# Spreading the running sums of a Mamba-2 head group over the partitions: matmuls into PSUM, or DMAs from a scratch in HBM

## The chip, the cores and the metric

The kernel runs on one core of a Trainium2 chip. The metric is the device time of one execution in microseconds (us), the median of several runs. The engines are TensorE (PE; its weight loads are listed apart as PEld), VectorE (DVE), ScalarE (ACT), GpSimd (POOL) and SyncE (SP), which here issues nearly all DMAs.

## The reference, cut to what matters

The model is a decoder trunk of two layers, 256 tokens, width 2048, in float32. Each layer normalises its input and projects it to the columns of an attention group and of a state-space (SSM) group; both outputs are normalised and mapped by one output projection.

```python
for l in range(DEPTH):                       # DEPTH = 2
    h = rmsnorm(x, norm_w)
    proj = h @ w_in                          # 2048 x 11856
    ... attention part (NSA), output y_attn ...
    xbc = silu(causal_depthwise_conv(xbc, conv_w, conv_b))
    xs, bm, cm = split(xbc)
    dt = softplus(dt + dt_bias); a = -exp(a_log)          # 32 heads
    # SSD, one chunk of 256 tokens, 8 groups of 4 heads
    cum   = cumsum(dt * a, axis=tokens)                   # (256, 32)
    decay = exp(where(causal, cum[l] - cum[s], -inf))     # (l, s, head)
    y = ((c @ b.T)[..., None] * decay) @ (xs * dt)
    y_ssm = grouped_rmsnorm((y + d_skip * xs) * silu(z), norm_ssm_w)
    x = x + concat(y_attn, y_ssm) @ w_out
return rmsnorm(x, final_norm_w)
```

The change is about `decay`: for each of 32 heads the kernel needs, on partition s and for all l, the difference of two running sums.

## The kernel before, in words

**Weight stream.** The weights of both projections are cut into tiles of 128 x 1024 (512 KB), 252 a layer. One tile is one *slot*. SyncE loads it into a ring of five buffers `wr` (line 147, issued in program order when VectorE has freed the oldest). ScalarE rounds it to `wh` (float32r, line 118), VectorE subtracts to get the rest `wl` (line 121); both run two slots ahead of TensorE (LH = LL = 2), each in a ring of four. In a slot TensorE (line 133) does eight pairs of matmuls: `wh` with 512 columns, then `wl` with 256. Two slots with 16 x 128 rows of input make one column tile in PSUM (`ppj`); it is evacuated in the next slot (`evac`, line 312).

**Side work.** All other work stands in generators that are resumed once per slot by `tick` (line 297); `yield from W(k)` lets WAITS[k] slots pass. So the order of the instructions on each engine is written out by hand, and a side instruction of TensorE stands between two slots of the stream.

**The SSM stage.** The column tiles come in the order `gd` (gates and dt), then for each of eight groups g: C, B, x, x, z, z, twelve slots a group. `gd_side` (line 369) makes dt, multiplies it by -exp(a_log) and takes the running sums by a matmul with a triangle (lines 409, 410): 32 heads on partitions, 256 tokens along them. It copies them to `cT` (tile `rt`) and, split into a rounded part and a rest, to the 64 rows of `cum2` (tile `PC`, lines 413 to 417); transposed they go to `cs`, 128 tokens on partitions. When the second z tile of group g is there, `ssm_side(g)` starts (line 816). It makes the products c b (`cb`, PSUM `b1`), transposes x (line 465), and then for each of its four heads spreads the running sums over all 128 partitions with a matmul: the stationary operand is a column of `eR`, a 64 x 32 pattern of ones, broadcast to 128 columns; the moving one is `cum2`; the result is `pc`, 4 x 256 columns in PSUM `b2` (line 471). ScalarE takes Relu(cs - pc) into `E` (tile `B`, a ring of two; lines 481, 482), then Exp of it; VectorE and GpSimd multiply by the masked `cb`; TensorE makes `py`, the last reader of `E` (line 495).

The lines that the change touches:

```python
cum2 = C["cum2"] = sb([96, 256], "PC", F32R)[0:64]
act(cum2[0:32], ps[0:32, :256])
lo(cum2[32:64], cT, cum2[0:32])
mm(pc[:, hh], eR[:, 4 * g + hh:4 * g + hh + 1].to_broadcast([64, 128]), C["cum2"], True, True)
act(E[:, hh, 0:256], pc[:, hh], AF.Relu, scale=-1.0, bias=cs[:, 0, c:c + 1])
```

The tag `B` also holds attention tiles later in the layer, and `PC` also an attention tile; `b2` also takes the sums of the compression and attention scores.

The other entries of the wait table that matter: from the start of `ssm_side` to its transposes 5 slots (W0 to W3), to the Relus 2 more (W5), to the Exp 2 (W9), to `py` 2 (W11); in `gd_side` the sums are copied in layer 0 at slot 18, in layer 1 earlier.

Of the kernel before, what the change touches and what calls it, by code (L numbers as in the profile page):

```python
# [11 lines left out]
F32 = mybir.dt.float32  # L12
F32R = mybir.dt.float32r
I32 = mybir.dt.int32
AF = mybir.ActivationFunctionType
# [70 lines left out]
def body(ctx: ExitStack, tc: tile.TileContext, wst, w1, xin, pos, w2, par, con, y):  # L86
    nc = tc.nc
# [3 lines left out]

    pp = ctx.enter_context(tc.tile_pool(name="pp", bufs=1))
    qq = ctx.enter_context(tc.tile_pool(name="qq", bufs=1, space=bass.MemoryType.PSUM))
    ctx.enter_context(tc.manual_schedule())

    cnt = [0]

    def sb(shape, tag, dt=F32, bufs=1):
        cnt[0] += 1
        return pp.tile(shape, dt, tag=tag, name=f"{tag}_{cnt[0]}", bufs=bufs)  # L100

    def pst(tag, shape=(128, 512), bufs=1):
        cnt[0] += 1
        return qq.tile(list(shape), F32, tag=tag, name=f"p{tag}_{cnt[0]}", bufs=bufs)

    def W(k):
        for _ in range(WAITS[k]):
            yield
# [3 lines left out]
    def act(out, in_, f=AF.Copy, **kw):  # L112
        if f in (AF.Ln, AF.Exp) and table[0] != AF.Exp:
            ACT.preload_act_table_set("natural_log_exp_and_others")  # L114
            table[0] = AF.Exp
        elif f in (AF.Silu, AF.Sin):
            table[0] = f
        ACT.activation(out, in_, f, **kw)  # L118
# [10 lines left out]
    def lo(out, full, hi):  # L129
        tt(out, full, f(hi), OP.subtract)  # L130

    def mm(out, lhsT, rhs, start, stop):
        PE.matmul(out, lhsT, rhs, start=start, stop=stop, skip_group_check=True)  # L133
# [67 lines left out]
    i4 = cst[:, C_I4:C_I4 + 32]  # L201
# [50 lines left out]

    one = sb([128, 1], "one", F32R)
    onr = one.to_broadcast([128, 128])
    eR = sb([64, 32], "eR", F32R)

    KT = [sb([128, 2, 2, 272], f"KT{g}", F32R) for g in range(2)]
    VC = [sb([96, 2, 128], f"VC{g}", F32R) for g in range(2)]
    PC = [None]
# [5 lines left out]
    cs = sb([128, 2, 32], "cs")  # L265
# [28 lines left out]
    sides = []  # L294
# [43 lines left out]
    h = [None] * NK  # L338
# [16 lines left out]
    for L in range(DEPTH):  # L355
# [4 lines left out]
        C = {}  # L360
# [8 lines left out]
        def gd_side(G):  # L369
# [2 lines left out]
            rmul(G)  # L372
            if L == 0:
                act(one, ones[:, 0:1])
                act(eR, i4[0:64])
            yield from W(27)
            if L == 0:
                sides.append(rope_tables())
# [29 lines left out]
            ps = pst("t", bufs=2)  # L408
# [1 line left out]
            mm(ps[0:32, 128:256], z[:, 1, :], tri, False, True)  # L410
            yield from W(36)
            cT = sb([128, 256], "rt")[0:32]
            cum2 = C["cum2"] = sb([96, 256], "PC", F32R)[0:64]
            act(cum2[0:32], ps[0:32, :256])
            act(cT, ps[0:32, :256])
            yield from W(37)
            lo(cum2[32:64], cT, cum2[0:32])
            ps = pst("t", bufs=2)
            for b in range(2):
                PE.transpose(ps[:, b * 32:b * 32 + 32], cT[:, b * 128:b * 128 + 128], ident[0:32, 0:32])  # L420
# [10 lines left out]
        def conv_side(U, dst, ct):  # L431
# [10 lines left out]
            for tap in (2, 1, 0):  # L442
                s = 3 - tap
                stt(dst[:, s:], U[:, :256 - s], w[:, tap:tap + 1], dst[:, s:], OP.mult, OP.add)

        def ssm_side(g, CV):
            yield from W(0)
            act(CV, CV, AF.Silu)
# [17 lines left out]
            yield from W(4)  # L466
            while "gd" not in C:
                yield
            pc = pst("b2", (128, 1024)).rearrange("p (h l) -> p h l", h=4)
            for hh in range(4):  # L470
                mm(pc[:, hh], eR[:, 4 * g + hh:4 * g + hh + 1].to_broadcast([64, 128]), C["cum2"], True, True)
            E = sb([128, 1536], "B", bufs=2).rearrange("p (h l) -> p h l", h=4)
            cbm = reg[:, 1536:1920]
            tt(cbm, cb[:, :384], mk3, OP.mult)
            xdt = reg[:, 2048:2560].rearrange("p (b h c) -> p b h c", b=2, h=4)
# [2 lines left out]
            yield from W(5)  # L478
            for hh in range(4):
                c = 4 * g + hh  # L480
                act(E[:, hh, 0:256], pc[:, hh], AF.Relu, scale=-1.0, bias=cs[:, 0, c:c + 1])
                act(E[:, hh, 256:384], pc[:, hh, 128:256], AF.Relu, scale=-1.0, bias=cs[:, 1, c:c + 1])
                if hh < 3:
                    yield from W(6 + hh)
            yield from W(9)
# [305 lines left out]
        def on_coltile(kind, i, ps):  # L791
# [21 lines left out]
            elif kind == "z":  # L813
                evac(ps, C["CV"][:, 4 + i % 2])
                if i % 2:
                    sides.append(ssm_side(i // 2, C["CV"]))
            elif kind in ("kc", "vc"):
                if i == 0 and kind == "kc":
                    C["w2"] = sb([128, 4, 128], "za")
# [241 lines left out]
```

## Time and profile before

| | |
|---|---|
| time, median of 3 runs | 1636.64 us (1636.07 to 1638.41) |
| profiled execution, first to last instruction (span) | 1634.5 us |
| TensorE busy | 1605.6 us, 98% |
| VectorE, ScalarE, GpSimd busy | 77%, 65%, 20% |
| DMA moved | 286.28 MB, mean 175 GB/s |
| DMA queue 1 (SyncE), share of 16 engines | 51.5% |

The profiled execution's own time is its span, 1634.5 us, and what lies before the first and after the last instruction, which the page does not list; the runs' median is 2.1 us above the span. Matmul durations are latencies and overlap, so how fast TensorE goes is read from start to start. A tile's name is followed by what it was made from: `pb<-PC,eR` is a matmul into PSUM `b2` that reads `PC` and `eR`. Names starting with p are PSUM.

### The profile page before, as it was taken

How to read it: one execution, taken by the hardware profiler on the slowest of the kernel's cores; microseconds unless marked ns; L12 is line 12 of the kernel's file. 1: busy time of each engine (PE TensorE's matmuls, PEld its weight loads, DVE VectorE, ACT ScalarE, POOL GpSimd, SP SyncE). 2: the span in 40 equal slices, each digit the busy share in tenths (PEclk: the TensorE clock that was granted, in tenths of full speed). 3: DMA queues.
4: the chain of work that ended last, by engine and by line, in shares of the span. 5: the costliest groups of instructions: out<-in, count | busy, mean ns of one | idle time of the engine just before them, and what ended most of it. 6: DMA issues, size and time to landing. Idle time of an engine off the chain costs nothing.

```text
span 1634.5 us, 26127 instructions
## 1 busy us (share of the span) xinstructions
PE 1605.6 (98%) x9590; PEld 1380.9 (84%) x9590; DVE 1263.6 (77%) x2224; ACT 1058.7 (65%) x1911; POOL 323.5 (20%) x342
## 2 busy tenths in 40 slices
PE   8999999999999999999999999999999999999996
PEld 6888888888888888888888888888788888888885
DVE  7878888877778788776677778788858878878654
ACT  5577767755677777545457777777557777765452
POOL 2222222221112222001112222222201212220011
PEclk8999999999999999999999999999999999999998
DMA  7545445477443444555555554545854443445552
GB/s 258 174 156 177 168 168 175 167 252 269 150 142 131 161 138 153 187 195 187 182 179 180 169 168 159 175 156 200 288 202 146 145 149 130 155 168 183 186 193 83
DMA packets 83777, 286.28 MB, mean 175 GB/s; under 512 B 9329, under 2 KB 9713, under 8 KB 83649
## 3 DMA queue, kind: packets, MB, share of 16 engines
q1 hardware_dynamic: 83376, 283.77, 51.5%
q8 instruction: 75, 1.23, 0.3%
q0 software_dynamic: 272, 0.84, 0.2%
q14 instruction: 54, 0.43, 0.1%
HBM read 282.48 MB, written 2.10 MB: 174 GB/s over the span
## 4 chain that ended last, share of the span: by engine, by line
PE 84%; ACT 8%; DVE 6%; issue 1%; DMA 1%; SPq 0%; DVEq 0%; ACTq 0%
PE ppj L133 75%; PE po L133 3%; PE pb L133 3%; ACT A L118 3%; ACT wh L118 2%; DVE wl L121 1%; DVE A L121 1%; ACT L114 1%; ACT L118 1%; PE pt L133 1%; DVE sm L121 1%; ACT PC L118 1%; DVE rt L121 1%; PE pt L465 0%; PE pt L726 0%
## 5 line engine op out<-in xcount | busy, mean ns | idle before, releaser
L121 DVE TENSOR_TENSOR wl<-wr,wh 128x1024 fp32r<-128x1024 f32 x503 | 624.6, 1251 | 206.3 <-ACT wh L118 205.6
L133 PE MATMUL ppj<-h,wh 128*128 128x512 f32 x1984 | 707.2, 400 | 7.7 <-DVE h L124 6.0
L133 PE MATMUL ppj<-s,wh 128*128 128x512 f32 x1984 | 703.1, 399 | 1.7 <-DVE za L121 1.7
L118 ACT ACTIVATE wh<-wr 128x1024 fp32r<-128x1024 f32 x503 | 522.4, 1047 | 112.0 <-PE ppj L133 89.2
L133 PE MATMUL ppj<-h,wl 128*128 128x256 f32 x1984 | 555.1, 280 | 0.0
L133 PE MATMUL ppj<-s,wl 128*128 128x256 f32 x1984 | 552.8, 279 | 0.0
L133 PEld LDWEIGHTS ppj<-h,wh 128*128 128x128 f32 x1984 | 373.4, 188 | 103.2 <-DVE h L124 7.9
L133 PEld LDWEIGHTS ppj<-s,wh 128*128 128x128 f32 x1984 | 372.4, 188 | 95.1 <-DVE za L121 3.3
L133 PEld LDWEIGHTS ppj<-h,wl 128*128 128x128 f32 x1984 | 375.1, 189 | 0.1
L133 PEld LDWEIGHTS ppj<-s,wl 128*128 128x128 f32 x1984 | 373.5, 188 | 0.1
L310 POOL TENSOR_TENSOR uu<-uu,rr 128x256 f32<-128x256 f32 x120 | 103.6, 864 | 576.3 <-DVE uu L121 555.3
L118 ACT ACTIVATE ev<-ppj 128x256 f32<-128x256 f32 x184 | 70.3, 382 | 189.1 <-PE ppj L133 184.9
L121 DVE TENSOR_TENSOR xT<-xT,ppj 128x256 f32<-128x256 f32 x128 | 53.8, 421 | 31.7 <-PE ppj L133 29.2
L118 ACT ACTIVATE A<-A,nm 128x128 f32<-128x128 f32 (+2 forms) x192 | 75.4, 394 | 0.9 <-DVE nm L661 0.4
L310 POOL TENSOR_TENSOR za<-za,rr 128x256 f32<-128x256 f32 x34 | 43.3, 1274 | 138.9 <-DVE za L121 115.4
L118 ACT ACTIVATE ev<-xT 128x256 f32<-128x256 f32 x30 | 12.6, 418 | 86.0 <-DVE xT L121 86.0
L121 DVE TENSOR_TENSOR uu<-ppj,ev 128x256 f32<-128x256 f32 x118 | 49.6, 420 | 23.6 <-ACT ev L118 22.9
L661 DVE CUSTOM_DVE_ANT_0 A<-pb,con 128x128 f32<-128x128 f32 (+2 forms) x192 | 44.1, 293 | 26.1 <-PE pt L729 25.6
L292 POOL TENSOR_TENSOR SQ<-SQ,ev 128x256 f32<-128x256 f32 x28 | 20.7, 741 | 218.8 <-ACT ev L118 218.8
L118 ACT ACTIVATE A<-A,sm 128x256 f32<-128x256 f32 x64 | 27.3, 498 | 46.9 <-DVE sm L121 46.9
L124 DVE SCALAR_TENSOR_TENSOR att<-uu,par,att 128x255 f32<-128x255 f32 (+2 forms) x96 | 55.6, 580 | 2.3
L124 DVE SCALAR_TENSOR_TENSOR A<-uu,par,A 128x255 f32<-128x255 f32 (+2 forms) x96 | 55.3, 576 | 2.3
(199 smaller groups left out, 1512.7 us busy)
## 6 DMA issues: line engine op xcount, KB each, us to landing
wr<-wst SPq DMA_DIRECT2D x500, 512.0 KB, 3.6
V<-w SPq DMA_DIRECT2D x64, 256.0 KB, 4.1
xT<-xin SPq DMA_DIRECT2D x4, 512.0 KB, 7.6
y<-xT SPq DMA_DIRECT2D x7, 256.0 KB, 2.9
za<-w POOLq DMA_DIRECT2D x2, 256.0 KB, 3.6
con<-con SPq DMA_DIRECT2D x1, 417.5 KB, 10.3
y<-xT SPq DMA_DIRECT2D x2, 128.0 KB, 1.7
par<-par SPq DMA_DIRECT2D x1, 184.0 KB, 3.6
```

Of the source, the lines that this page charges most:

```text
L114: ACT.preload_act_table_set("natural_log_exp_and_others")
L118: ACT.activation(out, in_, f, **kw)
L121: DVE.tensor_tensor(out, a, b, op=op)
L124: DVE.scalar_tensor_tensor(out, a, s, b, op0=op0, op1=op1)
L133: PE.matmul(out, lhsT, rhs, start=start, stop=stop, skip_group_check=True)
L292: POOL.tensor_tensor(sq[0], sq[0], t, op=OP.add)
L310: POOL.tensor_tensor(dst, dst, rr[0], op=OP.mult)
L661: DVE.tensor_tensor_reduce(out=o, in0=i, in1=m, op0=OP.add, op1=OP.min, scale=SC, scalar=3e38, accum_out=acc)
```

## The change

The running sums are written once per layer, as 32 rows of 256 floats, to a scratch in HBM (`cum`, 32 KB, a ring of two over the layers). For each group a new side `spread_side(g)`, started when the first x tile of the group is evacuated (slot 12g + 8 of the layer), waits until the scratch exists in the program and issues two DMAs on SyncE's queue straight into the group's `E`: the four rows of the group, read with a step of zero over the 128 partitions, 256 columns of each head, and then the last 128 columns again for the second block. `ssm_side` takes this `E`, and the Relus work in place. The four spreading matmuls, `eR`, `cum2` and `pc` go; `cT` and `cs` stay.

```diff
--- before.py
+++ after.py
@@ -91,6 +91,7 @@
 
     pp = ctx.enter_context(tc.tile_pool(name="pp", bufs=1))
     qq = ctx.enter_context(tc.tile_pool(name="qq", bufs=1, space=bass.MemoryType.PSUM))
+    dd = ctx.enter_context(tc.tile_pool(name="dd", bufs=1, space=bass.MemoryType.DRAM))
     ctx.enter_context(tc.manual_schedule())
 
     cnt = [0]
@@ -252,7 +253,6 @@
 
     one = sb([128, 1], "one", F32R)
     onr = one.to_broadcast([128, 128])
-    eR = sb([64, 32], "eR", F32R)
 
     KT = [sb([128, 2, 2, 272], f"KT{g}", F32R) for g in range(2)]
     VC = [sb([96, 2, 128], f"VC{g}", F32R) for g in range(2)]
@@ -372,7 +372,6 @@
             rmul(G)
             if L == 0:
                 act(one, ones[:, 0:1])
-                act(eR, i4[0:64])
             yield from W(27)
             if L == 0:
                 sides.append(rope_tables())
@@ -410,11 +409,10 @@
             mm(ps[0:32, 128:256], z[:, 1, :], tri, False, True)
             yield from W(36)
             cT = sb([128, 256], "rt")[0:32]
-            cum2 = C["cum2"] = sb([96, 256], "PC", F32R)[0:64]
-            act(cum2[0:32], ps[0:32, :256])
             act(cT, ps[0:32, :256])
+            cum = C["cum"] = dd.tile([32, 256], F32, tag="cum", name=f"cum_{L}", bufs=2)
+            nc.sync.dma_start(cum, cT)
             yield from W(37)
-            lo(cum2[32:64], cT, cum2[0:32])
             ps = pst("t", bufs=2)
             for b in range(2):
                 PE.transpose(ps[:, b * 32:b * 32 + 32], cT[:, b * 128:b * 128 + 128], ident[0:32, 0:32])
@@ -442,6 +440,19 @@
             for tap in (2, 1, 0):
                 s = 3 - tap
                 stt(dst[:, s:], U[:, :256 - s], w[:, tap:tap + 1], dst[:, s:], OP.mult, OP.add)
+
+        def spread(g):
+            E = C["E", g] = sb([128, 1536], "B", bufs=2).rearrange("p (h l) -> p h l", h=4)
+            cum = C["cum"]
+            for to, a, b in ((0, 0, 256), (256, 128, 256)):
+                src = bass.AP(tensor=cum.tensor, offset=cum.offset + 1024 * g + a,
+                              ap=[[0, 128], [256, 4], [1, b - a]])
+                nc.sync.dma_start(E[:, :, to:to + b - a], src)
+
+        def spread_side(g):
+            while "cum" not in C:
+                yield
+            spread(g)
 
         def ssm_side(g, CV):
             yield from W(0)
@@ -466,10 +477,7 @@
             yield from W(4)
             while "gd" not in C:
                 yield
-            pc = pst("b2", (128, 1024)).rearrange("p (h l) -> p h l", h=4)
-            for hh in range(4):
-                mm(pc[:, hh], eR[:, 4 * g + hh:4 * g + hh + 1].to_broadcast([64, 128]), C["cum2"], True, True)
-            E = sb([128, 1536], "B", bufs=2).rearrange("p (h l) -> p h l", h=4)
+            E = C["E", g]
             cbm = reg[:, 1536:1920]
             tt(cbm, cb[:, :384], mk3, OP.mult)
             xdt = reg[:, 2048:2560].rearrange("p (b h c) -> p b h c", b=2, h=4)
@@ -478,8 +486,8 @@
             yield from W(5)
             for hh in range(4):
                 c = 4 * g + hh
-                act(E[:, hh, 0:256], pc[:, hh], AF.Relu, scale=-1.0, bias=cs[:, 0, c:c + 1])
-                act(E[:, hh, 256:384], pc[:, hh, 128:256], AF.Relu, scale=-1.0, bias=cs[:, 1, c:c + 1])
+                act(E[:, hh, 0:256], E[:, hh, 0:256], AF.Relu, scale=-1.0, bias=cs[:, 0, c:c + 1])
+                act(E[:, hh, 256:384], E[:, hh, 256:384], AF.Relu, scale=-1.0, bias=cs[:, 1, c:c + 1])
                 if hh < 3:
                     yield from W(6 + hh)
             yield from W(9)
@@ -814,6 +822,8 @@
                 evac(ps, C["CV"][:, 4 + i % 2])
                 if i % 2:
                     sides.append(ssm_side(i // 2, C["CV"]))
+                else:
+                    sides.append(spread_side(i // 2))
             elif kind in ("kc", "vc"):
                 if i == 0 and kind == "kc":
                     C["w2"] = sb([128, 4, 128], "za")
```

## Rows read from the trace of the kernel before

**Rows 1.** The page's first part: busy us, share of the span, instructions.

```profile
PE 1605.6 (98%) x9590; PEld 1380.9 (84%) x9590; DVE 1263.6 (77%) x2224; ACT 1058.7 (65%) x1911; POOL 323.5 (20%) x342
```

**Rows 2.** Six groups as stretches, busiest and sum: busy us (x), PEclk, DMA share, GB/s.

```profile
151.87:189.50 37.63, 37.63 (x227) 32.23 (x225) 32.81 (x52) 27.49 (x43) 9.53 (x10) 1.00 0.52 168
...
sum 225.43, PE 225.43 PEld 193.21 DVE 188.64 ACT 168.13 POOL 55.24; mean PE 37.57 PEld 32.20 DVE 31.44 ACT 28.02 POOL 9.21
```

**Rows 3.** Chain of waits from 80 to 340 us, shares by line.

```profile
by line: PE ppj L133 90.8%; PE po L133 3.9%; PE pb L133 3.5%; PE pt L465 1.2%; PE pt L133 0.6%
```

**Rows 4.** All that reads eR: ns min/median/max, first and last start, form.

```profile
L133 PE MATMUL pb<-PC,eR x64: 271/276/383, 79.6 to 1140.4; 64*128 64x256 f32 x64
```

**Rows 5.** Timeline of TensorE, layer 0, group 0: start us, us, what.

```profile
79.02 0.27 PE L133 MATMUL ppj<-h,wl 128*128 128x256 f32 x1
...
79.36 0.28 PE L133 MATMUL ppj<-h,wl 128*128 128x256 f32 x1
79.58 0.72 PE L133 MATMUL pb<-PC,eR 64*128 64x256 f32 x4
...
80.57 0.28 PE L133 MATMUL ppj<-h,wl 128*128 128x256 f32 x1
```

**Rows 6.** Timeline of TensorE, the transposes of group 0.

```profile
76.24 0.62 PE L465 MATMUL pt<-con,A 128*128 128x128 f32 x4
...
76.94 0.28 PE L133 MATMUL ppj<-h,wl 128*128 128x256 f32 x1
```

**Rows 7.** Timeline of TensorE, the transposes of group 4.

```profile
226.79 0.62 PE L465 MATMUL pt<-con,A 128*128 128x128 f32 x4
227.35 0.73 PE L133 MATMUL pb<-PC,eR 64*128 64x256 f32 x4
...
228.34 0.28 PE L133 MATMUL ppj<-h,wl 128*128 128x256 f32 x1
```

**Rows 8.** Groups of ScalarE by shape: busy us, mean ns, idle before.

```profile
L118 ACT ACTIVATE ev<-ppj 128x256 f32<-128x256 f32 x184 | 70.3, 382 | 189.1 <-PE ppj L133 184.9 <-DVE att L393 1.9 <-DVE wl L121 1.9
...
L118 ACT ACTIVATE A<-A,nm 128x256 f32<-128x256 f32 x64 | 31.6, 495 | 0.0
L118 ACT ACTIVATE B<-pb,cs 128x256 f32<-128x256 f32 x64 | 31.3, 489 | 5.6 <-PE pb L133 5.6
...
L118 ACT ACTIVATE ev<-xT 128x256 f32<-128x256 f32 x30 | 12.6, 418 | 86.0 <-DVE xT L121 86.0
```

**Rows 9.** Who waited for whom, 114 to 340 us: total us, times, longest.

```profile
DVE wl L121 <- ACT wh L118: 21.1, 17, 3.0
```

**Rows 10.** DMA queues: 1624.4:1626.4 (q1), 17.5:18.1 and 17.5:19.3 us (q0): packets, MB, share.

```profile
q1 hardware_dynamic: 288, 0.26, 39.0%
...
q0 software_dynamic: 14, 0.06, 57.5%
...
q0 software_dynamic: 48, 0.13, 31.4%
```

**Rows 11.** Costliest conversions (mean ns of one), and SyncE's own waits.

```profile
L121 DVE TENSOR_TENSOR wl<-wr,wh 128x1024 fp32r<-128x1024 f32 x503 | 624.6, 1251 | 206.3 <-ACT wh L118 205.6
...
L118 ACT ACTIVATE wh<-wr 128x1024 fp32r<-128x1024 f32 x497 | 519.0, 1052 | 112.0 <-PE ppj L133 89.2 <-issue 20.0 <-DMA wr<-wst 2.3
...
SPq L147 <- DVE wl L121: 819.6, 307, 8.7
```

**Rows 12.** DMA queue 1 of the whole run, and issues: KB each, us to landing.

```profile
q1 hardware_dynamic: 83376, 283.77, 51.5%
...
wr<-wst SPq DMA_DIRECT2D x500, 512.0 KB, 3.6
...
y<-xT SPq DMA_DIRECT2D x2, 128.0 KB, 1.7
```

**Rows 13.** Timeline of ScalarE, layer 0: the running sums and the first Relus.

```profile
69.84 0.36 ACT L118 ACTIVATE rt<-pt 32x256 f32<-32x256 f32 x1
...
83.65 2.60 ACT L118 ACTIVATE B<-pb,cs 128x256 f32<-128x256 f32 x8
```

## The prediction

> **What bounds the kernel now.** The first part of the page says how much each engine works: TensorE is busy for 1605.6 of 1634.5 us, VectorE 77%, ScalarE 65% [rows 1]. Averages can hide stages, so the next view is the table of stretches over six SSM head groups, the stage that the change touches: TensorE is busy in every microsecond of 225.43, at the full granted clock (1.00, the 2.4 GHz level), while VectorE has 31.4 and ScalarE 28.0 us of work in a group's 37.6 [rows 2]. The chain of waits over the same stage has nothing but TensorE in it [rows 3]. So in this stage each microsecond taken out of TensorE's stream is a microsecond off the end, as long as nothing else becomes late, and work added elsewhere costs nothing as long as it stays inside its slack. That leaves two questions: what the removed matmuls cost as TensorE issues them, and whether the weights still come in time.
>
> **What goes from TensorE.** Per group and layer four matmuls `pb<-PC,eR` with 64 rows and 256 columns, 64 in all [rows 4]. Their durations (276 ns) are latencies that overlap their neighbours, so they must not be added up; what counts is how far the stream moves. I measure from one `wl` matmul to the next. In the undisturbed stream the period is 79.36 - 79.02 = 0.34 to 0.35 us. Across the four removed ones in group 0 it is 80.57 - 79.36 = 1.21 us [rows 5]. Excess: 0.86 us. A second pair of rows checks this. In group 0 the four transposes L465 go straight over into the stream, 0.70 us from the first of them to the next `wl` (76.24 to 76.94) [rows 6]; in group 4 the removed matmuls stand between, 1.55 us (226.79 to 228.34) [rows 7]. Difference: 0.85 us. 16 groups x 0.855 = 13.7 us.
>
> The rows also show where 0.855 comes from: from the first to the last start of the four it is about 0.72 - 0.27 = 0.45 us, and the other 0.4 lie around them, 0.22 ahead (79.36 to 79.58, where the stream's whole pair takes 0.34) and the rest behind [rows 5]. The Trainium skill, TensorEngine Tiling (Array Packing), Key Properties, says that changing the tiling mode drains the array; 64-row matmuls between 128-row ones are such a change, and the trace agrees with these longer steps at both ends.
>
> The Trainium skill, TensorE: Matmul & The Clock Gate, Back-to-back issue gap, prices a warm 256-column matmul at 262 cycles, 109 ns, and knows no gap at its ends; by that alone an estimate for 64 of them is 7.0 us and the time would be 1629.6.
>
> **What goes from ScalarE and VectorE.** Per layer one copy and one subtraction for `cum2`, and once the copy for `eR`. Neither engine is on the chain here [rows 3]: 0, with nothing to lose. The Relus' waits for `pb` (5.6 us in all) [rows 8] go too, also 0.
>
> **What is added to ScalarE.** The 128 Relus read SBUF where they read PSUM. The nearest rows bound it: with a pointer operand 128x256 takes 489 ns from PSUM (the Relu itself) and 495 from SBUF (`A<-A,nm`), so +6 ns; without, 382 from PSUM and 418 from SBUF, so +36 [rows 8]. That is 0.8 to 4.6 us over 16 groups, 0.05 to 0.3 a group. I take +6 ns, the row nearest in form. ScalarE has 37.6 - 28.0 = 9.6 us free in each group [rows 2]. Cost: 0.
>
> **What is added to SP and the DMA engines.** Per layer one store of 32 KB, per group two loads into `E`, 512 KB in pieces of 1 KB and 256 KB in pieces of 512 B: 786,432 B x 16 = 12.6 MB, beside 284 MB now. No row shows such a load, so it is bounded.
> Lower: the output stores move pieces of 1 KB; in their 2 us window queue 1 used 39.0% of 16 engines for 0.26 MB, 12.5 engine-us, so 786 KB take 37 engine-us, 2.3 us on all 16 [rows 10].
> Upper: the only load in which all partitions read the same bytes is that of the positions. In its worst 0.6 us, 14 packets took 57.5% of 16 engines, 5.5 engine-us for 57 KB, so 786 KB take 4.7 us; over its whole 1.8 us it is 9.0 engine-us for 131 KB, so 3.4 us [rows 10].
> I take 3.4, since that row shares the source pattern. Per group the engines then have 0.52 x 37.6 = 19.6 us of weights [rows 2] and 3.4 more: 61%.
>
> How late do weights get? SP issues a weight tile when VectorE's `lo` has freed its buffer [rows 11], and that tile is converted five conversions later, one per slot of 37.6 / 12 = 3.13 us: 15.7 us, less about 1.05 and 1.25 for the pair of conversions and up to 3.0 that `wl` waits for `wh` [rows 9, 11], less 3.6 us to landing [rows 12]: an estimate of 7 to 10 us of slack. ScalarE waits for a weight 2.3 us in the whole run [rows 11]. A spread in front puts 3.4 (at most 4.7) us and two issues into it. It stays inside; cost 0. If that cover were gone, each microsecond beyond it would stall the conversions first, and TensorE only after the two slots that they run ahead (LL = LH = 2).
>
> **The added waits on SP.** Behind a waiting spread stand the weight loads, so each wait matters.
> For the buffer: E(g) takes that of E(g-2), whose last reader, the `py` matmuls, runs at slot 12(g-2) + 25 = 12g + 1 by the wait table (an `ssm_side` starts at 12g + 14 and needs 11 more). The spread comes at slot 12g + 8: seven slots later, no wait.
> For the scratch: only the first spread of a layer is issued right behind the store. In layer 0 the copy `rt<-pt` ends at 70.20 us [rows 13]; a 128 KB store lands in 1.7 us [rows 12], so the 32 KB one in no more; SP stands still until about 72, then issues. The weight behind it comes about 2 to 3 us late, inside the 7 to 10. Bounds: 0 to 5 us once per layer on SP; I take 0 at the end.
> For the data: Relu of group 0 in layer 0 runs at 83.65 us [rows 13], spread issued by 73 and landed by about 80 even behind two weight tiles in flight. All others have 13 slots, 40 us.
>
> **Sum.** -13.7 + 0. The profiled execution's 1634.5 us become 1620.8. The median of the runs, 1636.64, lies 2.1 us above that span (what is outside first and last instruction); so 1622.9 us.
>
> **Rivals.**
> *The next engine takes part of the gain.* TensorE's group shrinks to 36.8 us, and VectorE with 31.4 (busiest group 32.8) in order behind ScalarE could be late at single slots. For: `wl` waits 21.1 us for `wh` in six groups [rows 9]. Against: those waits come from conversions running up to their ring, 37.6 - 32.8 = 4.8 us stay free in the busiest group. If half the gain goes: -6.8, 1629.8. Chance 0.11.
> *Columns only.* If the gaps at the ends stay, because the transposes meet the stream with a like gap, each group gives some 0.45 us: -7.2, 1629.4. Against it are rows 6, where transposes pass into the stream without one. Chance 0.04. The skill's 7.0 us above is near this.
> *Slower: the 16 DMA engines read one 4 KB block in turn.* All 128 partitions read the same four rows of the scratch. If they were served one packet at a time at the mean of queue 1, 51.5% x 16 x 1634.5 / 83376 = 162 ns per packet of up to 4 KB [rows 12], 192 such packets take 31 us per group. With 19.6 us of weights the group needs 50.7 us of DMA: 13.1 above 37.6, x 16 = +210, about 1846 us. It decides from the point where a spread takes more than the 7 to 10 us of slack. For: packets of the positions are slow at first. Against: served in turn the 128 KB of the positions, 32 such packets, would need 5.2 us; they all began within 1.8 [rows 10]. Chance 0.06. The Trainium skill, SBUF — State Buffer, section on the bandwidth-pool intuition, gives about 22.5 GB/s for one port of the HBM crossbar; if one port held the 4 KB, an estimate is 35 us per group, the same case.
> *No change.* The spreads delay the weights by just about the gain, or the first group of each layer waits 7 us for its data. Chance 0.05.
>
> **How the numbers follow.** Forecast 0.74, own range 1620.5 to 1625 (0.80 and 0.90 us a group as the ends of the reading, the spread of the runs, and up to 1 us for late first groups). Within 0.2%, 3.3 us, a measurement of this kernel shows no change. Faster: 0.74 + 0.11 + 0.04 = 0.89; same 0.05; slower 0.06. The range 1620.5 to 1630 takes in the partial gains and leaves out about 1 in 9.
>
> **What would show it.** No `pb<-PC,eR`; 0.70 us from the first transpose to the next `wl` in every group; groups 36.8 us long with TensorE still busy throughout; `E` loads of 512 and 256 KB landing in under 6 us; ScalarE's Relus 489 to 525 ns; no wait of `wh` for a weight above now's. Wrong would be: TensorE idle in this stage, weight loads landing after 10 us, or a group that stays at 37.6.

## The result, and the profile after

The changed kernel takes 1624.49 us (median of four runs, 1622.8 to 1625.3) against 1636.36 of the kernel before in the same set: ratio 0.9926 [0.9914, 0.9938], so it is 0.7% faster, little but clear of the noise. In a second set of runs it took 1629.41 us (five runs, 1625.72 to 1630.65) against 1635.74: 0.9951 [0.9937, 0.9964]. So the gain is 6 to 12 us, and the 5 us between the two sets of one and the same kernel have to be explained as well as the gain. (The second set ran on chip 2; the chip of the first is not on record. The kernel before agrees to 0.6 us between them.) The forecast was 1622.9, with a range of 1620.5 to 1630.

The profiled execution has a span of 1623.5 us where the one before had 1634.5: 11.0 us less. The page of the changed kernel, first the engines (busy us, share, instructions), then the DMA queue 1 (packets, MB, share of 16 engines) and the issues (KB each, us to landing):

```profile
PE 1593.9 (98%) x9526; PEld 1374.0 (85%) x9526; DVE 1264.9 (78%) x2222; ACT 1062.5 (65%) x1908; POOL 329.7 (20%) x342
...
q1 hardware_dynamic: 100368, 296.42, 54.0%
...
wr<-wst SPq DMA_DIRECT2D x500, 512.0 KB, 3.6
...
B<-cum SPq DMA_DIRECT2D x16, 512.0 KB, 4.7
B<-cum SPq DMA_DIRECT2D x16, 256.0 KB, 6.4
```

Against [rows 1] TensorE lost 64 matmuls and 11.7 us of busy time, and the other engines gained 1 to 6 us. Queue 1 got 16,992 packets and 12.65 MB more, its share went from 51.5% to 54.0% [rows 12]; a weight tile still lands in 3.6 us.

The stage of the change, six groups as in [rows 2] (columns as there):

```profile
149.76:186.24 36.48, 36.48 (x222) 31.63 (x222) 32.80 (x52) 27.74 (x43) 9.83 (x10) 1.00 0.57 195
...
296.51:332.99 36.48, 36.48 (x223) 31.65 (x222) 30.09 (x41) 26.63 (x41) 10.03 (x11) 1.00 0.69 231
sum 220.02, PE 220.02 PEld 190.10 DVE 189.70 ACT 169.41 POOL 58.21; mean PE 36.67 PEld 31.68 DVE 31.62 ACT 28.24 POOL 9.70
```

TensorE is still busy in every microsecond of the stage, a group has shrunk from 37.57 to 36.67 us, VectorE's and ScalarE's work is what it was. In the second of the six groups the DMA share rose from 0.52 to 0.57.

TensorE's timeline where the matmuls stood (start us, us, what), groups 0 and 4:

```profile
76.08 0.63 PE L476 MATMUL pt<-con,A 128*128 128x128 f32 x4
...
76.77 0.28 PE L134 MATMUL ppj<-h,wl 128*128 128x256 f32 x1
...
223.13 0.63 PE L476 MATMUL pt<-con,A 128*128 128x128 f32 x4
...
223.83 0.28 PE L134 MATMUL ppj<-h,wl 128*128 128x256 f32 x1
```

Group 4 needs 0.70 us from the first transpose to the next `wl`, as group 0 did before [rows 6]; it needed 1.55 [rows 7].

The new loads, all 32 of them (what the issue takes on SP's queue in ns, then us from issue to landing), and the Relus by shape (busy us, mean ns | idle before):

```profile
L450 SPq DMA_DIRECT2D B<-cum x32: 377/498/1233, 75.4 to 1108.5; - x32
...
DMA to landing us min/median/max: 3.8/5.4/7.6
```

```profile
L119 ACT ACTIVATE B<-B,cs 128x256 f32<-128x256 f32 x64 | 31.8, 498 | 0.0
L119 ACT ACTIVATE B<-B,cs 128x128 f32<-128x128 f32 x64 | 25.0, 390 | 0.0
```

The 128x256 Relu went from 489 to 498 ns [rows 8], and its wait for data from 5.6 us to none. ScalarE waits for no spread in this execution, but SyncE waits for the scratch: in each layer the first spread stands in the queue until the store has landed. The queue's waits (total us, times, longest), its issues in layer 0 and the first Relus behind them:

```profile
SPq L450 <- DMA cum<-rt: 7.8, 2, 3.9
```

```profile
71.11 0.42 SPq L414 DMA_DIRECT2D cum<-rt  x1
75.45 0.93 SPq L450 DMA_DIRECT2D B<-cum  x2
...
82.67 1.48 ACT L119 ACTIVATE B<-B,cs 128x256 f32<-128x256 f32 x4
```

The store of 32 KB took 4.3 us to land in both layers. Layer 0's first spread has landed at 82.1 us, 0.6 us before the first Relu that reads it.

**Where the 11.0 us come from.** Both executions have the same 9526 matmuls apart from the removed ones, in the same order, so they can be laid side by side, start against start. Each step from one start to the next is put into one of four classes:

```
span difference, us            after  second set   no spread  waits[43]=2
                                      (profile)    (e4)       (e7)
place of the removed matmuls  -13.64    -13.64      -13.66     -13.65
the weight stream itself       +2.13     +6.31       +3.54      -0.95
idle time of TensorE           +1.12     +1.89       +0.87      -0.29
other side work, ends          -0.63     -0.22       +0.04      -1.86
sum                           -11.02     -5.66       -9.21     -16.75
```

The first line is the same in all to 0.02 us: that is what the change takes out. The other lines decide between 5.7 and 16.8. Of these the second and the fourth share a border that can be drawn in more than one way (up to 1.3 us between them); and the kernel before, profiled again (b0_before), differs from its own first profile by -1.3 us, in the last three lines, so differences of that size say nothing.

**The line "idle time".** In each layer the last group is followed by the attention stage, and there TensorE now waits. The changed kernel, TensorE (idle before it in brackets):

```profile
340.01 1.07 PE L134 MATMUL pb<-V,B 128*32 128x256 f32 x16 [0.74 <-DVE B L122]
```

Before, these sixteen followed the stream at 346.38 us with 0.05 us of idle time. VectorE makes their operand in a chain that does not get shorter when TensorE's groups do, so most of one group's saving goes back there, 0.74 us in either layer.

**The line "stream".** A pair of `wh` and `wl` in the undisturbed stream takes one of two times. The kernel before in layer 0's output projection, and then the changed one at the same place:

```profile
699.92 0.39 PE L133 MATMUL ppj<-s,wh 128*128 128x512 f32 x1
...
700.26 0.40 PE L133 MATMUL ppj<-s,wh 128*128 128x512 f32 x1
...
700.62 0.39 PE L133 MATMUL ppj<-s,wh 128*128 128x512 f32 x1
...
700.96 0.40 PE L133 MATMUL ppj<-s,wh 128*128 128x512 f32 x1
```

```profile
699.80 0.40 PE L134 MATMUL ppj<-s,wh 128*128 128x512 f32 x1
...
700.15 0.40 PE L134 MATMUL ppj<-s,wh 128*128 128x512 f32 x1
...
700.50 0.40 PE L134 MATMUL ppj<-s,wh 128*128 128x512 f32 x1
...
700.86 0.40 PE L134 MATMUL ppj<-s,wh 128*128 128x512 f32 x1
```

Three pairs in 1.04 us against three in 1.06. It looks like rounding, but the mean over 430 pairs of the stage is 346.7 ns before and 353.3 after (the fast and the slow rhythm below), with the same instructions, no idle time and the granted clock at 1.00. The two output projections have 430 and 415 such pairs at 6.6 ns: the stages are 2.9 and 2.8 us longer in the slow rhythm. In these executions the stream keeps, between two side matmuls, the rhythm with which it was entered. Both also occur in the SSM stage, before the change too: there 46 pairs from 80.2 us on take 353.5 ns each, 46 from 265.6 us on 346.7. Which rhythm each layer's output projection had in each profile (mean ns of a pair):

```
                          layer 0  layer 1
before, three profiles     346.7    346.7     (the first, b0_before, e11_before_U)
after, first set           353.3    346.7
after, second set          353.3    353.3     (e0_again)
e1, e2, e3, e10            353.3    353.3
e4, e5                     346.7    353.3
e8                         353.3    346.7
e7                         346.7    346.7
e9                         347.0    347.0
```

### The profile page after: what moved, and what is told of

It reads as the page before. It is cut to its first block, busy times and chain, and to the rows that moved or that the text cites. A ratio compares the mean times of both kernels' runs of the same rounds, so it can differ in the third digit from the quotient of the medians.

```text
span 1623.5 us, 26084 instructions
## 1 busy us (share of the span) xinstructions
PE 1593.9 (98%) x9526; PEld 1374.0 (85%) x9526; DVE 1264.9 (78%) x2222; ACT 1062.5 (65%) x1908; POOL 329.7 (20%) x342
## 4 chain that ended last, share of the span: by engine, by line
PE 84%; ACT 8%; DVE 6%; issue 1%; DMA 0%; DVEq 0%; SPq 0%; ACTq 0%
PE ppj L134 75%; PE po L134 4%; ACT A L119 3%; PE pb L134 3%; DVE wl L122 2%; ACT wh L119 2%; DVE A L122 1%; ACT L115 1%; ACT L119 1%; PE pt L134 1%; DVE sm L122 1%; ACT PC L119 1%; DVE rt L122 1%; PE pt L476 0%; PE pt L734 0%
## 5 line engine op out<-in xcount | busy, mean ns | idle before, releaser
L119 ACT ACTIVATE A<-A,nm 128x128 f32<-128x128 f32 (+2 forms) x192 | 75.4, 394 | 0.9 <-DVE nm L669 0.4
L122 DVE TENSOR_TENSOR uu<-ppj,ev 128x256 f32<-128x256 f32 x118 | 49.5, 419 | 17.8 <-ACT ev L119 16.8
L125 DVE SCALAR_TENSOR_TENSOR att<-uu,par,att 128x255 f32<-128x255 f32 (+2 forms) x96 | 59.5, 620 | 2.3
```

The costliest lines, as they stand in the source:

```text
L122: DVE.tensor_tensor(out, a, b, op=op)
L125: DVE.scalar_tensor_tensor(out, a, s, b, op0=op0, op1=op1)
```

## The experiments

The theory: TensorE alone sets the pace; the four matmuls cost 0.855 us per group, of which 0.4 are a price of their 64 rows that is paid once per visit; the spreads stay inside the slack of the weights and are free. Rivals: the matmuls' price is that of columns, and the rest comes from elsewhere; the spreads do cost something, which a larger gain hides; the new wait at the hand-over, or the rhythm, is the price of the spreads.

All ratios are against the kernel before, run in turn with it on the same chip: chip 2, but chip 4 for e8 to e11, where the changed kernel itself was not run. The kernel before takes 1635.7 to 1635.8 us on either.

**The kernel again (e0_again).** No edit.

> The changed kernel once more, nothing edited. In the first profile of it TensorE's eight pairs of a slot follow each other every 353.3 ns throughout the output projection of layer 0 (664 to 826 us), in the profile of the kernel before every 346.7 ns, with the same instructions; that alone is 3.0 us. Theory A: this rhythm is picked anew in each execution when the stream is re-entered after a side matmul; then the runs spread by about 3 us (1621 to 1625.5) and the new profile may show the other rhythm, with a span of about 1620.5 us if it does. Theory B: the rhythm belongs to the instruction sequence of this kernel; then the profile shows 353.3 ns there again and runs stay within 1 us of 1624.5.

1629.41 us, 0.9951 [0.9937, 0.9964]. Neither theory's time came true: layer 0 shows the slow rhythm again, as theory B has it, but the time is not that of the first set. The table above tells its profile apart from the first: the same 13.64 us at the place of the change, and 2.8 us lost to the slow rhythm in layer 1's output projection too. The five runs lie between 1625.72 and 1630.65, a spread nearly as large as two steps of 2.8; the kernel before has 1634.55 to 1636.99 in 25 runs.

**The price of the matmuls (e1_four64, e2_one64, e3_four128).** Matmuls that nothing reads, put back at the same place, with the spreads left as they are: four with 64 rows, one with 64, four with 128.

```diff
                 yield
+            pc = pst("b2", (128, 1024)).rearrange("p (h l) -> p h l", h=4)
+            for hh in range(4):                       # e2: range(1)
+                mm(pc[:, hh], one[0:64].to_broadcast([64, 128]), h[0][0:64, 0:256], True, True)
             E = C["E", g]                             # e3: 128 rows instead of 64
```

> The changed kernel, with four matmuls of 64 rows and 256 columns per group put back on TensorE where the spreading ones stood; nobody reads their result, the spreads by DMA stay. Main theory (the gain is TensorE's stream and the DMAs cost nothing): +0.855 us in 14 groups and about 0.1 in the last group of each layer, +12 us, 1636.5 us, level with the kernel before. Rival (the DMAs cost the part of the gain that is missing, some 1.7 us): all 13.7 us come back on top, 1638.2 us.

> As the run with four, but one matmul of 64 rows per group. If the price of the four is half columns (0.11 us each) and half gaps at the two ends (0.40 us), one costs 0.5 us in 14 groups: +7 us, 1631.5 us. If there is no price at the ends, one costs a quarter of 0.855: +3 us, 1627.5 us.

> As the run with four, but over 128 rows, as all its neighbours in the stream. If the gaps come from going from 128 to 64 rows and back, only the columns are left: 4 x 0.117 = 0.47 us in 14 groups, +6.6 us, 1631 us. If any four matmuls there cost the same, +12 us, 1636.5 us.

Measured: 1640.58 us, 1.0027 [1.0018, 1.0037]; 1635.25, 0.9992 [0.9984, 1.0001]; 1637.54, 1.0008 [0.9999, 1.0016]. As times these three mislead: none came out as expected (e3's lies nearest to the other reading's 1636.5), since the expectations start from 1624.5 us, and in their profiles all three ran both output projections in the slow rhythm, 5.7 us that the kernel before does not pay. Against the second set of the changed kernel, whose profile pays both too, they are 11.2, 5.8 and 8.1 us longer, where 12, 7 and 6.6 were expected. The timelines of TensorE in group 0 show the price itself. Four of 64 rows:

```profile
78.49 0.28 PE L134 MATMUL ppj<-h,wl 128*128 128x256 f32 x1
78.70 0.73 PE L134 MATMUL pb<-h,one 64*128 64x256 f32 x4
...
79.69 0.28 PE L134 MATMUL ppj<-h,wl 128*128 128x256 f32 x1
```

One of 64 rows:

```profile
79.98 0.28 PE L134 MATMUL ppj<-h,wl 128*128 128x256 f32 x1
80.19 0.38 PE L134 MATMUL pb<-h,one 64*128 64x256 f32 x1
...
80.84 0.28 PE L134 MATMUL ppj<-h,wl 128*128 128x256 f32 x1
```

Four of 128 rows:

```profile
80.00 0.28 PE L134 MATMUL ppj<-h,wl 128*128 128x256 f32 x1
80.11 0.63 PE L134 MATMUL pb<-h,one 128*128 128x256 f32 x4
...
80.81 0.28 PE L134 MATMUL ppj<-h,wl 128*128 128x256 f32 x1
```

From `wl` to `wl` 1.20, 0.86 and 0.81 us; less a pair's 0.35 that is 0.85, 0.51 and 0.46. Over all 16 groups, laid side by side as above, 13.61, 8.04 and 7.47 us more than without them: 0.851, 0.503 and 0.467 a group. So a 256-column matmul costs 0.117 us in the stream, and going from 128 rows to 64 and back costs another 0.39, once for one as for four: 0.39 + 4 x 0.117 = 0.86. At 128 rows the 0.39 is gone. The rows see it at both ends: 0.21 us from the last `wl` to the first of the 64-row ones, where 128-row ones need 0.11, and the rest behind. The reading "columns only" falls. The same runs show whose time goes back at the hand-over: where the changed kernel idles 0.74 us there, these idle 0.04, 0.28 and 0.32 us in each layer, the less the more of the group's saving is put back.

**The kernel before, again (b0_before).** No edit.

> The kernel before once more, nothing edited, for its profile. In its first profile the stream ran at 346.7 ns a pair in both output projections; in the five profiles of the changed kernel and its variants it ran at 353.3 in that of layer 0 every time and in that of layer 1 four times. If the rhythm is drawn anew in each execution, this profile may show either, and its span differs from 1634.5 us by up to 6. If it follows from the instruction sequence, it shows 346.7 in both again, with a span within 1.5 us of 1634.5; then the changed kernel's sequence loses some 3 us at each output projection, and the gain is smaller than the matmuls removed for that reason.

1635.74 us, 0.9998 [0.9988, 1.0007], and the fast rhythm in both output projections, as in the first profile of it; the span of 1633.2 us is within the 1.5 of "follows from the instruction sequence". The changed kernel's layer 1 has shown both rhythms from one sequence, though, so that theory is not the whole of it.

**Without the spreads (e4_no_spread).** The 128 Relus read a tile that is in SBUF anyway; the store to the scratch stays.

```diff
-            E = C["E", g]
+            E = sb([128, 1536], "B", bufs=2).rearrange("p (h l) -> p h l", h=4)
...
-                act(E[:, hh, 0:256], E[:, hh, 0:256], AF.Relu, scale=-1.0, bias=cs[:, 0, c:c + 1])
-                act(E[:, hh, 256:384], E[:, hh, 256:384], AF.Relu, scale=-1.0, bias=cs[:, 1, c:c + 1])
+                act(E[:, hh, 0:256], CV[:, hh], AF.Relu, scale=-1.0, bias=cs[:, 0, c:c + 1])
+                act(E[:, hh, 256:384], CV[:, hh, 128:256], AF.Relu, scale=-1.0, bias=cs[:, 1, c:c + 1])
...
-                else:
-                    sides.append(spread_side(i // 2))
```

> The changed kernel without the spreads: E is made where it was made before, and the Relus read the convolved tile (any SBUF data of the same shape) in place of the spread sums; the store to the scratch stays. Main theory (the spreads cost nothing): the time of the changed kernel on this chip, 1629.4 us, give or take the rhythm's 3 us; the removed matmuls give the same 13.6 us. Rival (the DMAs cost time by holding up weights or VectorE): 2 to 3 us faster than that, the mean of the convolution's 128x255 operations on VectorE falls from 612 back to 578 ns, and the two waits of 0.74 us at the start of the compression go.

1626.11 us, 0.9941 [0.9929, 0.9954], between the two results of the full change. The place of the removed matmuls gives the same 13.66 us, and at the hand-over to the attention stage TensorE still idles as long, in both layers:

```profile
340.32 1.07 PE L134 MATMUL pb<-V,B 128*32 128x256 f32 x16 [0.74 <-DVE B L122]
```

The time alone, 3.3 us below the second set, would suit the rival too; but 2.9 us of it are layer 0's output projection in the fast rhythm. The rival's other signs stayed away: the waits are there, and the convolution's operations on VectorE take 612 ns on average as in the changed kernel (578 before). With the four matmuls put back (e1) they take 577 although the spreads are there, so what slows them is not the loads; what it is stays open. Without the two output projections the run lies 12.0 us below the kernel before, and the two profiles of the full change 13.9 and 11.3. So the spreads cost nothing that can be told from the noise, and the wait at the hand-over does not come from them.

**More loads into the same tile (e5_spread4).** Each spread is issued four times.

```diff
-            for to, a, b in ((0, 0, 256), (256, 128, 256)):
+            for to, a, b in 4 * ((0, 0, 256), (256, 128, 256)):
```

> The changed kernel with each pair of spread loads issued four times over (the same data to the same place). Estimate from its trace: one spread is 512 packets of 1 KB at 46 ns and 512 of 512 B at 27 ns, 2.3 us on 16 engines; four are 9.3 us, with 19 us of weights 28 of a group's 36.7. The weights behind them come 7 us later than in the changed kernel, where they have 5 to 8 us to spare: the conversions lose a few us once per group and catch up, TensorE has two slots in hand: within 1 us per layer, 1629 to 1632 us. Rival (the weights' slack is what decides, no reserve behind it): 1 to 3 us in each of 16 groups, 1645 us or more.

1748.35 us, 1.0682 [1.0667, 1.0696]: 7 us more per group, on the rival's side (1645 us or more). But this is not the price of bytes alone. SyncE's own waits, whole run, and then those of the conversions, 100 to 340 us (total us, times, longest):

```profile
SPq L450 <- DMA B<-cum: 182.8, 95, 4.9
```

```profile
ACT wh L119 <- DMA wr<-wst: 38.5, 5, 10.1
```

Here a load that overwrites what an earlier one wrote waits in the queue, by a semaphore, until that one has landed, 1.9 us each on average, and the weights stand behind it. So the experiment mixed two causes; the next one parts them.

**More loads, each into a tile of its own (e10_load3).** Two more of 512 KB and three of 256 KB per group, from the same scratch, into tiles that are free in this stage: three times the bytes. (The three went out in all 16 groups, where the expectation speaks of 15.)

```diff
+            for j in range(2):
+                src = bass.AP(tensor=cum.tensor, offset=cum.offset + 1024 * g, ap=[[0, 128], [256, 4], [1, 256]])
+                nc.sync.dma_start(f(KT[j].rearrange("p a b c -> p (a b) c")[:, :, 0:256]), src)
+            for j in range(3):
+                src = bass.AP(tensor=cum.tensor, offset=cum.offset + 1024 * g, ap=[[0, 128], [256, 4], [1, 128]])
+                nc.sync.dma_start(sb([128, 512], "V", bufs=4).rearrange("p (h l) -> p h l", h=4), src)
```

> The changed kernel with more bytes read from the scratch for each group, into tiles that are idle in this stage, so that no load waits for an earlier one: two more loads of 512 KB in pieces of 1 KB and (in 15 of the 16 groups) three more of 256 KB in pieces of 512 B; nobody reads them. 2.5 MB a group in place of 0.79, by the packets' 46 and 27 ns about 7.9 us of all 16 engines in place of 2.3. Theory A (in the run with the spreads issued four times over it was the waits in SP's queue, each load for the landing of the one before, that stopped the weights, not the bytes): the weights land up to 5.6 us later once per group, inside what they have to spare and the two slots in hand: 1626 to 1632 us. Theory B (the bytes did it): +3 to 7 us in 16 groups, 1680 to 1740 us.

1667.13 us, 1.0194 [1.0177, 1.0211]: between the two theories and in the range of neither. Its issues on the page, and the chain of waits over three groups (start us, us, what):

```profile
wr<-wst SPq DMA_DIRECT2D x500, 512.0 KB, 4.1
KT<-cum SPq DMA_DIRECT2D x32, 512.0 KB, 7.8
...
V<-cum SPq DMA_DIRECT2D x48, 256.0 KB, 9.2
```

```profile
140.09 9.99 DMA wr<-wst
...
179.11 9.25 DMA wr<-wst
...
219.18 9.09 DMA wr<-wst
```

Once per group a weight tile takes 9 to 10 us to land, because the loads in front share the 16 engines with it (busy share 1.01 from 135 to 150 us). That is what the slack of the weights could not take: TensorE idles 25 us more than in the kernel before, and 14 go to the stream, 5.7 of them in the two output projections and 6 in four places of the SSM stage where the granted clock was 0.50; the next experiment shows such a place. So the spread is free at its own size and not at three times it. The room is smaller than it looked: from landing to its conversion a weight tile had 4.3 us at least and 7.4 to 8.5 at the median (by stretches of 40 us, 80 to 310 us) before, and 4.2 and 6.4 to 7.6 after.

**The spread issued late (e8_late_spread).** It is issued where the matmuls stood, right in front of the Relus, instead of eleven slots earlier.

```diff
+            spread(g)
             E = C["E", g]
...
-                else:
-                    sides.append(spread_side(i // 2))
```

> The changed kernel with the two spread loads of a group issued where the spreading matmuls stood, in the side that uses them, two slots (5.7 us) before the first Relu, in place of 13 slots before. In the changed kernel they land 4.7 and 6.4 us after issue, so the Relus should wait 1 to 2 us in each group. Theory A: ScalarE has 9 us free in a group and TensorE two slots in hand, so nothing reaches the end: within 2 us of the changed kernel on this chip, 1627 to 1631 us. Theory B: a late Relu holds the evacuations and conversions behind it on ScalarE and TensorE waits: +1 to 2 us in 16 groups, 1645 to 1660 us.

1674.21 us, 1.0228 [1.0211, 1.0245]: slower than the kernel before and than theory B's 1645 to 1660, by the same bytes that are free when issued early. Who waited for whom, 100 to 340 us, and a piece of its chain:

```profile
DVE wl L122 <- ACT wh L119: 42.5, 23, 5.1
ACT B L119 <- DMA B<-cum: 35.1, 12, 5.5
```

```profile
195.20 5.19 DMA B<-cum
200.72 2.17 ACT B L119 x6
203.38 0.96 ACT wh L119
204.37 1.23 DVE wl L122
```

ScalarE waits for the landing, up to 5.5 us of it, and the conversion `wh` stands behind the Relus on the same engine; `wl` follows, then TensorE, which gains 33 us of idle time over the 16 groups. The stream loses another 15 us, which no theory had. Two stretches (columns as in [rows 2]):

```profile
244.00:247.00 3.00, 0.65 (x4) 0.38 (x3) 1.99 (x4) 3.00 (x4) 0.39 (x1) 1.00 0.01 4
248.00:251.00 3.00, 3.00 (x11) 2.52 (x11) 3.00 (x3) 2.93 (x6) 0.67 (x1) 0.50 0.34 138
```

TensorE stands idle, and then works at a granted clock of 0.50, the 1.2 GHz level. That happened at six places of the SSM stage, each time during or right behind 2.1 to 3.5 us of idle time, 27 us in all; the steps of the stream in them took 11.5 us longer than before. 3 us more are layer 0's slow rhythm. In the stage of the kernel before and of the changed one the clock never left 1.00. So what the spread needs is not bandwidth but a lead as long as its landing time, and where it is missing, more is lost than the waits.

**The wait at the hand-over (e7_U_early, e11_before_U).** One entry of the wait table starts VectorE's chain for the attention stage one slot earlier, in the changed kernel and, separately, in the kernel before.

```diff
-WAITS = [..., 1, 1, 3, 4, 0, ...]
+WAITS = [..., 1, 1, 2, 4, 0, ...]      # WAITS[43]
```

> The changed kernel with one entry of the wait table one slot shorter (W43, 3 to 2): VectorE prepares the operand of the compression's matmuls a slot earlier. In the changed kernel TensorE waits 0.74 us for it once per layer, which is the saving of the last group of each layer given back. Main theory: both waits go, -1.5 us against the changed kernel on this chip (1629.4), other things (the rhythm) equal. Rival: VectorE is full there, the work only moves and delays a conversion; no change.

> The kernel before with the same entry of the wait table a slot shorter (W43, 3 to 2). There TensorE did not wait for the compression's operand, so nothing should be gained: 1635.7 us, within 1 us. Rival: the earlier preparation is worth 1.5 us or more by itself, 1634 us or less, and what the changed kernel gained from it is not a wait that the change brought.

In the changed kernel 1620.99 us, 0.9908 [0.9895, 0.9922], the fastest of all versions; in the kernel before 1635.27, 0.9995 [0.9985, 1.0004]. The first of the two, TensorE at the hand-over of layer 0:

```profile
338.00 1.07 PE L134 MATMUL pb<-V,B 128*32 128x256 f32 x16
```

No idle time in front of it any more, and the class "idle" went from +1.12 to -0.29: 1.4 us, as expected. The whole gain was larger than the 1.5 expected: of the profile's 5.7 us against the first one of the changed kernel 2.9 are rhythm, since both output projections ran in the fast one (5.7 of 11.1 against the second), and 1.4 (3.2) are scattered and unexplained. Before the change the same edit is worth nothing, so the wait was made by the change.

**The rhythm (e9_flip).** One matmul with 128 rows and 256 columns that nothing reads, put into each output projection.

```diff
                 yield
+                mm(pst("b1")[:, 0:256], onr, Q[0][:, 0], True, True)
                 for k in range(NK + 2):
```

> The changed kernel with one more matmul (128 rows, 256 columns, read by nobody) put between two slots right at the start of each output projection. In the two profiles of the changed kernel the stream of layer 0's output projection ran at 353.3 ns a pair both times. Theory A: the rhythm is set where the stream is re-entered after a side matmul and holds until the next one; the extra matmul sets it anew, and if it comes out at 346.7 in layer 0 that stage is 2.9 us shorter, 1.5 to 6 us in all below 1629.4. If it comes out at 353.3 again, the time is 1629.5 and the run does not decide. Theory B: the rhythm belongs to the stage (its operands, its addresses); then it stays at 353.3 in layer 0.

1623.08 us, 0.9923 [0.9908, 0.9937]. In the trace the extra matmul does not stand in front of the projection, but behind its first 22 pairs, in layer 0 here:

```profile
672.59 0.28 PE L134 MATMUL pb<-Q,one 128*128 128x256 f32 x1
```

The 22 pairs before it take 353.1 ns each, the 407 behind it 346.7; in layer 1 it is the same, 22 at 353.1 and 392 at 346.7. With one matmul more than the changed kernel, layer 0's stage is 2.6 us shorter, as theory A has it (the time lies 6.3 below 1629.4, where 1.5 to 6 were expected). So one matmul turned the rhythm from slow to fast inside a stage, twice in one execution: it does not belong to the stage. What decides which rhythm is taken up is not shown: layer 1's was fast without it in one profile of the changed kernel and slow in the other.

## Why the prediction was right, and where it was off

*TensorE alone bounds the stage.* Right: busy in all of 220.02 us after, as in [rows 2].

*13.7 us from the matmuls.* Right: 13.64 at that place in each of four executions. The two ways of reading it, from `wl` to `wl` and against a group whose transposes run straight on, gave it to 0.1 us, because they use starts in the stream and not durations. Its split, 0.45 for columns and 0.4 for ends, was right too (0.47 and 0.39). The Trainium skill, TensorEngine Tiling (Array Packing), Key Properties, says that a change of tiling mode drains the array; the runs with 64 and 128 rows agree with it, and add the number, 0.39. The 7.0 us by the Trainium skill's TensorE: Matmul & The Clock Gate, Back-to-back issue gap, was half of what came: its 109 ns a matmul is near the 117 in the stream, but has no ends.

*ScalarE and VectorE at nothing.* Right at the end: +9 ns a Relu where +6 was taken. That the convolution on VectorE would take 34 ns more per operation was not foreseen.

*The spread at nothing.* Right at this size, shown by leaving it out (the same wait at the hand-over, nothing gained elsewhere but rhythm) and by tripling it (not free). The landing of 3.8 to 7.6 us lay above the "under 6" that was to show it; why is not shown; it shares the engines with weights. The rival that 128 partitions reading the same 4 KB are served in turn falls: the 786 KB of a group had landed 8.0 us after their first issue at worst, where that rival had 31 us, and the estimate from the port figure of the Trainium skill, SBUF — State Buffer, section on the bandwidth-pool intuition, 35.

*The store and the first spread.* Here the end is right and the steps are not. A 32 KB store was to land in no more than 1.7 us, as one of 128 KB does; it took 4.3, and SyncE stood still for 3.9 us in each layer, inside the bounds of 0 to 5. So layer 0's first spread went out at 75.4 us and not by 73, and had landed 0.6 us before its Relu where some 3.6 were counted on. In e7 and e9 the Relus did wait for it, 0.8 us. That it cost nothing owes something to luck.

*The weights' slack of 7 to 10 us.* The median was in it before (7.4 to 8.5), the least was not: 4.3. An estimate from a mean slot cannot give the least. It did no harm: the least after the change is 4.2, so the spread hardly took from it; with more loads in front of the weights it would have misled, as the tripled loads do.

*"The next engine takes part of the gain", 6.8 us at 0.11.* It happened, smaller and elsewhere: not at single slots inside the stage, but at its end, 0.74 us once in each layer, where TensorE meets a chain of VectorE with a fixed start in slots. The prediction asked what is late next only inside the stage.

*The sum.* 1623.5 of span against 1620.8 forecast. The step that is missing is the 2.1 us of the stream, beside the 1.1 of idle time: the sum took it that the untouched stages keep their time. They didn't, by 2.9 us in layer 0's output projection, and in the profile of the second set by 2.8 more in layer 1's. The profile of the kernel before has both rhythms, 353.5 ns in the stretch from 80.2 us on and 346.7 in the output projections, so the size of a switch could be read from it, where the prediction names one period of 0.34 to 0.35 us; that these stages would switch could not be read. So it is partly luck that the first set came within 1.6 us of the forecast's 1622.9: the second lies 6.5 above it, at the time of the two rivals with partial gains (1629.4 and 1629.8) and for neither's reason.

What stays open is what sets the rhythm when the stream is entered, and so how many of the 5.7 us any one execution of the changed kernel pays.

## What to carry to other kernels

Measure a removed matmul from start to start in the stream and look for the price at its ends: a visit of 64-row matmuls to a 128-row stream cost 0.39 us however many there were, so four at 128 rows were cheaper than one at 64. A broadcast through DMA is free only with a lead of its landing time (5 to 8 us here for both loads of a group) and as long as the loads behind it on the same queue keep their slack; the same bytes issued late, or three times over, made this kernel slower than before. When one engine's stage shrinks, look at the hand-over to the next stage, where another engine's chain still starts at its old slot.

## What the runs showed of the hardware

The same stream of matmuls (512 and 256 columns in turn) ran at 346.7 or at 353.3 ns a pair, at the full granted clock and without idle time, for hundreds of pairs on end. One more matmul in the stream turned the slow rhythm into the fast one (e9). In the fast one the steps from start to start repeat after two pairs (113, 232, 118, 230 ns), in the slow one after three (113, 233, 117, 241, 120, 236).

Loads that give all 128 partitions the same bytes took a median of 46 ns of an engine for a packet of 1 KB, as the 1 KB packets of the output stores did, and 27 ns for one of 512 B, so a spread is 2.3 us of 16 engines, the lower bound of the prediction, and not the 3.4 taken from the positions.

Idle time of TensorE cost more than itself: behind waits of 2.1 to 3.5 us in the late-spread run the granted clock fell from 1.00 to 0.50 six times, and the stream lost 11.5 us there beside the 33 us of idle time.
